# One row of a residual RMSNorm's second tile, dealt out unevenly to the DMA engines in patches of single partitions

## Chip, cores, metric

One core of one Trainium2 chip. The metric is the device time of one execution in microseconds (us), the median of several runs; runs of one kernel here mostly agree within 0.3%.

## The reference

```python
# x, residual: (32, 2048, 2048) float32; gamma: (2048,); eps = 1e-6
z = x + residual
rms = np.sqrt(np.mean(z ** 2, axis=-1, keepdims=True) + eps)
return (z / rms * gamma).astype(np.float32)
```

There are 65,536 rows of 8 KB. Each is read twice (x and residual) and written once: 1.61 GB in all.

## The kernel before

Rows go through in tiles of 128 partitions. Tile 0 has three rows in each partition, tile 1 five, and 72 further tiles seven each. Two buffers `z` (x, then the sum, then the result) alternate, and `r_area` holds residuals. SyncE issues every transfer; VectorE adds and scales; ScalarE squares and sums. GpSimd only clears the semaphores at the end.

```python
lead = [3, 5]
sizes = lead + [R] * n_full                       # R = 7
def rows(t, i):                                   # tile i of an HBM tensor
    k = sizes[i]
    return t[starts[i] : starts[i] + P * k, :].rearrange("(p r) m -> p r m", r=k)
...
def sp_turn(sp, t):                               # SyncE, for each tile i
    t.wait(sp, "done", -1)                        # tile i-1 computed
    ... dma_start(out=rows(o_f, i - 1), in_=z[...])        # store it
    t.wait(sp, "add_a")                           # first add of tile i done
    load_r(sp, t, 1)                              # residual of tile i+1
    t.wait(sp, "s_out", -1)                       # the store has landed
    load_x(sp, t, 1)                              # x of tile i+1
...
def sync_program(sp):
    load_x(sp, Turn(0)); load_r(sp, Turn(0))
    sp.wait_ge(tail_ev["add"], 1)                 # a memset of the gamma stage
    ... four loads of gamma
    load_r(sp, Turn(1)); load_x(sp, Turn(1))
    for i in range(1, n_tiles): sp_turn(sp, Turn(i))
    ... the last tile's stores, in four parts
```

Of the kernel before, what the change touches and what calls it, by code (L numbers as in the profile page):

```python
# [9 lines left out]
def kernel(  # L10
# [14 lines left out]



    nc = tc.nc
    P = nc.NUM_PARTITIONS
    fp32 = mybir.dt.float32  # L30
# [3 lines left out]
    x_f = x.flatten_outer_dims()  # L34
    r_f = residual.flatten_outer_dims()
    o_f = out.flatten_outer_dims()

    n_rows, D = x_f.shape
    R = 7
    STEP = 4  # L40
    U = 16
    lead = [3, 5]
    n_full = (n_rows // P - sum(lead)) // R
    sizes = lead + [R] * n_full
    starts = [0]
    for k in sizes:
        starts.append(starts[-1] + P * k)
    assert starts[-1] == n_rows
    n_tiles = len(sizes)
    last = n_tiles - 1  # L50

# [5 lines left out]
    def rows(t, i):  # L57
        k = sizes[i]
        return t[starts[i] : starts[i] + P * k, :].rearrange("(p r) m -> p r m", r=k)

    inv_d = 1.0 / float(D)

    def sb(name, shape):
        return ctx.enter_context(nc.sbuf_tensor(name, shape, fp32))
# [4 lines left out]
    sems = []  # L69

    def sem(name):
        sems.append(ctx.enter_context(nc.semaphore(name)))
        return sems[-1]
# [3 lines left out]
    z = [sb(f"z{p}", [P, R, D]) for p in range(2)]  # L77
    r_area = sb("r_area", [P, R + STEP, D])
    eps_tile = sb("eps_tile", [P, 1])
    ssq = [[sb(f"ssq{p}{h}", [P, 4]) for h in range(2)] for p in range(2)]  # L80
    rms = [[sb(f"rms{p}{h}", [P, 4]) for h in range(2)] for p in range(2)]
    rstd = [[sb(f"rstd{p}{h}", [P, 4]) for h in range(2)] for p in range(2)]
    tail_ssq = sb("tail_ssq", [P, R])
    tail_rms = sb("tail_rms", [P, R])
    tail_rstd = sb("tail_rstd", [P, R])
# [8 lines left out]
    dve = sem("dve_own")  # L94
    act = sem("act_own")
    s_tail = sem("s_tail")
    fin = sem("fin")
    tail_ev = {k: sem(f"tail_{k}") for k in ("add", "rms", "done")}


# [2 lines left out]
    def entry(i):  # L103
        if i == 0:
            return R + STEP - sizes[0]
        return 0 if i % 2 else STEP

    def parts(i):
        if i == 0:
            return [(0, 2), (2, sizes[0])]  # L110
        k = sizes[i] if i < 2 else R
        return [(STEP, k), (0, STEP)] if i % 2 else [(0, R - STEP), (R - STEP, R)]

    class Turn:

# [12 lines left out]
    def inc(ins, kind, i):  # L128
        return ins.then_inc(ev[kind][i % 2], U)


    def load_x(sp, t, d=0):
        i = t.i + d
        inc(sp.dma_start(out=z[i % 2][:, : sizes[i], :], in_=rows(x_f, i)), "x_in", i)

    def load_r(sp, t, d=0):
        i = t.i + d
        e = entry(i)
        inc(
            sp.dma_start(out=r_area[:, e : e + sizes[i], :], in_=rows(r_f, i)),  # L140
            "r_in",
            i,
        )

    def sp_turn(sp, t):
        i = t.i
        t.wait(sp, "done", -1)
        inc(
            sp.dma_start(out=rows(o_f, i - 1), in_=z[(i - 1) % 2][:, : sizes[i - 1], :]),
            "s_out",  # L150
            i - 1,
        )
        if i == last:
            return
        t.wait(sp, "add_a")
        load_r(sp, t, 1)
        t.wait(sp, "s_out", -1)
        if i + 1 == last:
            for k, (a, b) in enumerate(tail):
                sp.dma_start(  # L160
                    out=z[last % 2][:, a:b, :], in_=rows(x_f, last)[:, a:b, :]
                ).then_inc(x_tail[k], U)
        else:
            load_x(sp, t, 1)


    def add(v, i, a, b):
        e = entry(i)
        s = z[i % 2][:, a:b, :]
        return v.tensor_add(out=s, in0=s, in1=r_area[:, e + a : e + b, :])  # L170

    def scale(v, i, a, b, rs, c=0):
        for g in range(a, b):
            s = z[i % 2][:, g, :]
            ins = v.scalar_tensor_tensor(  # L175
                out=s,
                in0=s,
                scalar=rs[:, c + g - a : c + g - a + 1],
                in1=gamma_tile[:, :],
                op0=mult,  # L180
                op1=mult,
            )
        return ins

    def dve_turn(v, t, own):
        i, p = t.i, t.p
        t.wait(v, "x_in")
        t.wait(v, "r_in")
        (a0, b0), (a1, b1) = parts(i)
        inc(add(v, i, a0, b0), "add_a", i)  # L190
        inc(add(v, i, a1, b1), "add_b", i)
        for h, (a, b) in enumerate(parts(i)):
            n = b - a
            t.wait(v, "rms_a" if h == 0 else "rms_b")
            v.reciprocal(out=rstd[p][h][:, :n], in_=rms[p][h][:, :n]).then_inc(dve, U)  # L195
            v.wait_ge(dve, own(i, h))
            ins = scale(v, i, a, b, rstd[p][h])
        inc(ins, "done", i)
# [44 lines left out]



    stage = r_area[:, 5:7, :].rearrange("p r m -> p (r m)")
    stage = stage.rearrange("p (a b) -> p a b", a=16)[:, :, : D // 16]

    def sync_program(sp):
        load_x(sp, Turn(0))  # L250
        load_r(sp, Turn(0))

        sp.wait_ge(tail_ev["add"], 1)
        for q in range(4):
            sp.dma_start(  # L255
                out=stage[32 * q : 32 * q + 1],
                in_=gamma.partition_broadcast(1).rearrange("p (a b) -> p a b", a=16),
            ).then_inc(g_in, U)
        load_r(sp, Turn(1))
        load_x(sp, Turn(1))  # L260
        for i in range(1, n_tiles):
            sp_turn(sp, Turn(i))
        for k, (a, b) in enumerate(tail):
            sp.wait_ge(tail_ev["done"], k + 1)
            sp.dma_start(
                out=rows(o_f, last)[:, a:b, :], in_=z[last % 2][:, a:b, :]
            ).then_inc(s_tail, U)

    def vector_program(v):
        v.memset(eps_tile[:, :], float(eps))  # L270
        v.memset(stage, 0.0).then_inc(tail_ev["add"], 1)  # L271
        v.wait_ge(g_in, 4 * U)
        v.stream_shuffle(gamma_tile[:, :].rearrange("p (a b) -> p a b", a=16), stage, [0] * 32)  # L273
        for i in range(LO):
            dve_turn(v, Turn(i), lambda i, h: (2 * i + h + 1) * U)
        with v.Fori(0, 2 * n_iter, 2) as it:
            for i in range(LO, LO + 2):
                dve_turn(v, Turn(i, it), lambda i, h: it * (2 * U) + (2 * i + h + 1) * U)
        for i in range(HI, last):
            dve_turn(v, Turn(i), lambda i, h: (2 * i + h + 1) * U)  # L280
        base = 2 * last * U
        t = Turn(last)
        t.wait(v, "r_in")

        def tail_scale(k):
            a, b = tail[k]
            v.wait_ge(tail_ev["rms"], k + 1)
            v.reciprocal(out=tail_rstd[:, a:b], in_=tail_rms[:, a:b]).then_inc(dve, U)  # L288
            v.wait_ge(dve, base + (k + 1) * U)
            scale(v, last, a, b, tail_rstd, a).then_inc(tail_ev["done"], 1)  # L290

        for k, (a, b) in enumerate(tail):
            v.wait_ge(x_tail[k], U)
            add(v, last, a, b).then_inc(tail_ev["add"], 1)
            if k:
                tail_scale(k - 1)
        tail_scale(len(tail) - 1)

    def scalar_program(s):
        chain = Chain(s, act)  # L300
        for i in range(LO):
            act_turn(s, Turn(i), chain)
        with s.Fori(0, 2 * n_iter, 2) as it:
            n = chain.n
            chain.base = it * R
            for i in range(LO, LO + 2):
                act_turn(s, Turn(i, it), chain)
            assert chain.n - n == 2 * R
        chain.base = None
        chain.n = n + 2 * R * n_iter  # L310
        for i in range(HI, last):
            act_turn(s, Turn(i), chain)
        for k, (a, b) in enumerate(tail):
            chain.wait()
            s.wait_ge(tail_ev["add"], k + 2)
            act_part(
                s, chain, z[last % 2], a, b, tail_ssq[:, a:b], tail_rms[:, a:b]
            ).then_inc(tail_ev["rms"], 1)

    sync_program(nc.sync)  # L320
    vector_program(nc.vector)
    scalar_program(nc.scalar)

    nc.gpsimd.wait_ge(ev["s_out"][(last - 1) % 2], ((last - 1) // 2 + 1) * U)
    nc.gpsimd.wait_ge(s_tail, U * len(tail))
    ids = [a.num for a in sems]
    assert ids == list(range(ids[0], ids[0] + len(ids)))
    nc.gpsimd.sem_clear(range(ids[0], ids[-1] + 1))


# [33 lines left out]
```

## Time and profile before

| | before |
|---|---|
| time, median (lowest to highest of 3) | 3726.32 us (3726.11 to 3726.45) |
| VectorE / ScalarE / GpSimd busy | 62% / 29% / 0% |
| DMA traffic over the span | 432 GB/s mean, 434 in mid-run |
| last stores: first and last of the final sixteen semaphore increments | 3717.03 and 3723.36 us |

The trace of before has sixteen increments of the semaphore for each transfer of 128 partitions (592 for the 37 loads of x into `z[0]`), and they are read here as one from each of the core's sixteen DMA engines when its share has landed. The trace also keeps one record for each packet (a packet here is the contiguous rows of one partition: 24 KB in tile 0, 40 KB in tile 1, 56 KB later) with its duration, but not the engine of a packet. One more table of stretches is needed. Its columns are the stretch, its length, busy time of VectorE, ScalarE and GpSimd (with instructions), the granted TensorE clock, the mean busy share of the DMA engines, and GB/s. The kernel before:

```profile
16.00:40.00 24.00, 16.01 (x9) 7.77 (x9) 0.00 (x0) 1.00 1.01 429
40.00:60.00 20.00, 13.31 (x4) 7.93 (x8) 0.00 (x0) 1.00 1.03 442
60.00:350.00 290.00, 180.42 (x62) 82.04 (x92) 0.00 (x0) 1.00 1.00 433
350.00:3600.00 3250.00, 2008.80 (x705) 934.74 (x1022) 0.00 (x0) 1.00 1.00 434
```

A share near 1 says that the engines always had a packet in hand. (A packet counts in the stretch in which it starts, so a share can pass 1.)

### The profile page before, as it was taken

To read this page: it belongs to the slowest core of one execution; us is meant where nothing else is said; L and a number is where in the kernel's file an instruction comes from. 1 tells how busy PE (TensorE), PEld (TensorE's weight loads), DVE (VectorE), ACT (ScalarE), POOL (GpSimd) and SP (SyncE) were. 2 spreads that over 40 slices of the span, in tenths; PEclk is the share of its full clock that TensorE was granted. 3 is DMA by queue.
4 is the path that set the end of the run, shared out by engine and by line. 5 is a ranking of instruction groups with operands and counts; after the bars stand their busy time and mean duration, and the time that the engine had idled before them with its cause. 6 is when DMAs were issued, how large, how long until landed. Compare 5 with 4: busy or idle time off the path is not lost.

```text
span 3724.5 us, 3677 instructions
## 1 busy us (share of the span) xinstructions
DVE 2302.6 (62%) x816; ACT 1072.4 (29%) x1176; POOL 0.2 (0%) x4
## 2 busy tenths in 40 slices
DVE  5666665566665566665566665566665566655566
ACT  2233322233322233322233322233322233322233
POOL 0000000000000000000000000000000000000000
DMA  9999999999999999999999999999999999999999
GB/s 421 431 434 434 433 434 436 434 434 434 434 434 434 434 434 434 434 434 434 434 434 434 434 434 434 434 434 434 434 434 434 434 434 434 434 434 434 434 433 399
DMA packets 32964, 1610.69 MB, mean 432 GB/s; under 512 B 3712, under 2 KB 3776, under 8 KB 3776
## 3 DMA queue, kind: packets, MB, share of 16 engines
q1 hardware_dynamic: 32960, 1610.66, 99.9%
q14 instruction: 4, 0.03, 0.0%
HBM read 1073.77 MB, written 536.87 MB: 432 GB/s over the span
## 4 chain that ended last, share of the span: by engine, by line
DMA 66%; DVE 22%; issue 10%; ACT 1%; SPq 0%; DVEq 0%; ACTq 0%
DMA out_dram<-z 33%; DMA z<-in_x_dram 33%; DVE z L170 15%; DVE z L175 7%; ACT sq_junk L221 1%; DMA r_area<-in_gamma_dram 0%; ACT rms L229 0%; DVE rstd L195 0%; DVEq L126 0%; SPq L255 0%; DVE r_area L271 0%; ACTq L209 0%; ACTq L126 0%; DVE tail_rstd L288 0%; SPq L160 0%
## 5 line engine op out<-in xcount | busy, mean ns | idle before, releaser
L170 DVE TENSOR_TENSOR z<-z,r_area 128x8192 f32<-128x8192 f32 (+2 forms) x150 | 1109.5, 7437 | 1253.0 <-DMA z<-in_x_dram 1226.8
L221 ACT ACTIVATE sq_junk<-z 128x2048 f32<-128x2048 f32 x512 | 963.4, 1882 | 2617.9 <-DVE z L170 2606.5
L175 DVE SCALAR_TENSOR_TENSOR z<-z,rstd,gamma_tile 128x2048 f32<-128x2048 f32 x505 | 1153.5, 2344 | 5.2
L195 DVE RECIPROCAL rstd<-rms 128x4 f32<-128x4 f32 (+2 forms) x146 | 25.3, 174 | 130.8 <-ACT rms L229 130.8
L221 ACT ACTIVATION_READ_ACCUMULATOR sq_junk<-z 128x1 f32 x512 | 95.4, 186 | 0.0
L229 ACT ACTIVATE rms<-ssq,eps_tile 128x4 f32<-128x4 f32 (+2 forms) x146 | 43.3, 297 | 13.4
L175 DVE SCALAR_TENSOR_TENSOR z<-z,tail_rstd,gamma_tile 128x2048 f32<-128x2048 f32 x7 | 16.2, 2346 | 0.1
L273 DVE LOAD_MASK_SELECT gamma_tile<-r_area x1 | 0.0, 14 | 16.4 <-DMA r_area<-in_gamma_dram 16.4
L273 DVE STREAM_SHUFFLE gamma_tile<-r_area 128x2048 f32<-128x2048 f32 x1 | 2.3, 2290 | 0.0
L271 DVE MEMSET r_area<- 128x2048 f32 x1 | 1.8, 1765 | 0.4 <-issue 0.4
L221 ACT ACT_TABLE_LOAD x1 | 1.3, 1283 | 0.9 <-SPq L75 0.9
L229 ACT ACT_TABLE_LOAD x1 | 1.3, 1283 | 0.1
L229 ACT ACTIVATE tail_rms<-tail_ssq,eps_tile 128x2 f32<-128x2 f32 (+1 forms) x4 | 1.2, 295 | 0.1
L270 DVE MEMSET eps_tile<- 128x1 f32 x1 | 0.1, 59 | 1.0 <-SPq L75 1.0
L288 DVE RECIPROCAL tail_rstd<-tail_rms 128x2 f32<-128x2 f32 (+1 forms) x4 | 0.6, 158 | 0.0
L345 POOL MEMSET const-bfloat16-1.0<- 128x1 bf16 x1 | 0.1, 102 | 0.0
L345 POOL MEMSET const-uint8-127<- 128x1 uint8 x1 | 0.1, 102 | 0.0
L345 POOL MEMSET const-float32-1.0<- 128x1 f32 x1 | 0.1, 99 | 0.0
L345 POOL MEMSET const-float32-0.0<- 128x1 f32 x1 | 0.1, 98 | 0.2 <-issue 0.2
## 6 DMA issues: line engine op xcount, KB each, us to landing
r_area<-in_residual_dram SPq DMA_DIRECT2D x72, 7168.0 KB, 27.2
z<-in_x_dram SPq DMA_DIRECT2D x71, 7168.0 KB, 33.8
out_dram<-z SPq DMA_DIRECT2D x71, 7168.0 KB, 34.4
z<-in_x_dram SPq DMA_DIRECT2D x3, 2048.0 KB, 26.3
out_dram<-z SPq DMA_DIRECT2D x3, 2048.0 KB, 14.1
r_area<-in_residual_dram SPq DMA_DIRECT2D x1, 5120.0 KB, 25.3
z<-in_x_dram SPq DMA_DIRECT2D x1, 5120.0 KB, 36.8
out_dram<-z SPq DMA_DIRECT2D x1, 5120.0 KB, 24.8
```

The costliest lines, as they stand in the source:

```text
L170: return v.tensor_add(out=s, in0=s, in1=r_area[:, e + a : e + b, :])
L175: ins = v.scalar_tensor_tensor(out=s, in0=s, scalar=rs[:, c + g - a : c + g - a + 1], in1=gamma_tile[:, :], op0=mult, op1=mult,)
L195: v.reciprocal(out=rstd[p][h][:, :n], in_=rms[p][h][:, :n]).then_inc(dve, U)
L221: s.activation(out=sq_junk[:, :], in_=src[:, g, :], func=Act.Square, accum_out=sq[:, g - a : g - a + 1],)
L229: return s.activation(out=rm, in_=sq[:, : b - a], func=Act.Sqrt, bias=eps_tile[:, :], scale=inv_d)
L270: v.memset(eps_tile[:, :], float(eps))
L271: v.memset(stage, 0.0).then_inc(tail_ev["add"], 1)
L273: v.stream_shuffle(gamma_tile[:, :].rearrange("p (a b) -> p a b", a=16), stage, [0] * 32)
L288: v.reciprocal(out=tail_rstd[:, a:b], in_=tail_rms[:, a:b]).then_inc(dve, U)
L345: nc = _bacc.Bacc("TRN2", target_bir_lowering=False, num_devices=1)
```

## The change

Its intent: some DMA engines end later than others, so give them fewer rows. Tile 1 keeps four rows in every partition. Its fifth row (128 rows of HBM) is dealt out in six patches. A patch `(e, n, j, r)` puts `r` rows into each of the `n` partitions `8e + j`, `8(e+1) + j`, and so on, eight apart, so that each is meant for one DMA engine. (The patch families lie on partitions two apart, `j` = 0, 2, 4.) SyncE issues three patches; GpSimd issues three, with tiny loads between them that are meant to turn the engine at which the next patch begins. Partitions without a patch hold zeros.

```diff
-    lead = [3, 5]
+    lead = [3, 4]
+    sp_patches = [(0, 16, 0, 3), (0, 4, 2, 3), (0, 3, 4, 3)]
+    pool_patches = [(5, 2, 4, 1), (8, 8, 4, 3), (5, 11, 2, 3)]
+    def patch_rows(t, q):                 # the patch's rows in HBM, one after the other
+        n = first_row[q]
+        return t[n : n + q[1] * q[3], :].rearrange("(p r) m -> p r m", r=q[3])
+    def patch(area, q):                   # its place in SBUF
+        e, n, j, r = q
+        p = 8 * e + j
+        return area[p : p + 8 * (n - 1) + 1 : 8, STEP : STEP + r, :]
 ...
+        for k, t, area in ((0, r_f, r_area), (1, x_f, z[1])):       # SyncE
+            sp.wait_ge(clean[k], 1)       # memset of three rows
+            for q in sp_patches:
+                sp.dma_start(out=patch(area, q), in_=patch_rows(t, q)).then_inc(m_in, U)
         load_r(sp, Turn(1))
         load_x(sp, Turn(1))
 ...
+                if n:                     # GpSimd: meant to turn the engine
+                    g.dma_start(out=tiny[:n, c], in_=x_f[:n, c]).then_inc(t_in[turn], U)
+                move(m, q)                # load, later store, of one patch
```

VectorE's first add of tile 1 waits for the patches alone. The store of tile 1 is followed by the patches' stores. (Left out: semaphores, a reset of GpSimd's queue, and gamma's stage, which moves from `r_area` to `z[0]`.)

More of the change, by code (lines that the diff above doesn't have):

```diff
@@ L41 @@
     U = 16
-    lead = [3, 5]
-    n_full = (n_rows // P - sum(lead)) // R
+    lead = [3, 4]
+    n_full = (n_rows // P - sum(lead) - 1) // R
     sizes = lead + [R] * n_full
     starts = [0]
-    for k in sizes:
-        starts.append(starts[-1] + P * k)
+    for i, k in enumerate(sizes):
+        starts.append(starts[-1] + P * k + (P if i == 1 else 0))
     assert starts[-1] == n_rows
+    sp_patches = [(0, 16, 0, 3), (0, 4, 2, 3), (0, 3, 4, 3)]
+    pool_patches = [(5, 2, 4, 1), (8, 8, 4, 3), (5, 11, 2, 3)]
+    first_row = {}
+    n = starts[1] + P * sizes[1]
+    for q in sp_patches + pool_patches:
+        first_row[q] = n
+        n += q[1] * q[3]
+    assert n == starts[2]
     n_tiles = len(sizes)
@@ L82 @@
     rstd = [[sb(f"rstd{p}{h}", [P, 4]) for h in range(2)] for p in range(2)]
+    tiny = sb("tiny", [16, 64])
     tail_ssq = sb("tail_ssq", [P, R])
@@ L96 @@
     s_tail = sem("s_tail")
-    fin = sem("fin")
+    clean = [sem(f"clean{k}") for k in range(2)]
+    m_in = sem("m_in")
+    m_out = sem("m_out")
+    n_q = len(pool_patches)
+    q_in = [sem(f"q_in{k}") for k in range(2 * n_q)]
+    q_out = [sem(f"q_out{k}") for k in range(n_q)]
+    t_in = [sem(f"t_in{k}") for k in range(3 * n_q)]
     tail_ev = {k: sem(f"tail_{k}") for k in ("add", "rms", "done")}
@@ L110, in parts @@
             return [(0, 2), (2, sizes[0])]
-        k = sizes[i] if i < 2 else R
-        return [(STEP, k), (0, STEP)] if i % 2 else [(0, R - STEP), (R - STEP, R)]
+        return [(STEP, R), (0, STEP)] if i % 2 else [(0, R - STEP), (R - STEP, R)]
     class Turn:
@@ L152, in sp_turn @@
         )
+        if i == 2:
+            for q in sp_patches:
+                sp.dma_start(out=patch_rows(o_f, q), in_=patch(z[1], q)).then_inc(m_out, U)
         if i == last:
@@ L157, in sp_turn @@
         t.wait(sp, "s_out", -1)
+        if i == 2:
+            sp.wait_ge(m_out, len(sp_patches) * U)
+            for k in q_out:
+                sp.wait_ge(k, U)
         if i + 1 == last:
@@ L186, in dve_turn @@
         i, p = t.i, t.p
-        t.wait(v, "x_in")
-        t.wait(v, "r_in")
+        if i == 1:
+            v.wait_ge(m_in, 2 * len(sp_patches) * U)
+            for k in q_in:
+                v.wait_ge(k, U)
+        else:
+            t.wait(v, "x_in")
+            t.wait(v, "r_in")
         (a0, b0), (a1, b1) = parts(i)
         inc(add(v, i, a0, b0), "add_a", i)
+        if i == 1:
+            t.wait(v, "x_in")
+            t.wait(v, "r_in")
         inc(add(v, i, a1, b1), "add_b", i)
@@ L242, in act_turn @@
             )
-    stage = r_area[:, 5:7, :].rearrange("p r m -> p (r m)")
+    stage = z[0][:, 3:5, :].rearrange("p r m -> p (r m)")
     stage = stage.rearrange("p (a b) -> p a b", a=16)[:, :, : D // 16]
@@ L258, in sync_program @@
             ).then_inc(g_in, U)
+        for k, t, area in ((0, r_f, r_area), (1, x_f, z[1])):
+            sp.wait_ge(clean[k], 1)
+            for q in sp_patches:
+                sp.dma_start(out=patch(area, q), in_=patch_rows(t, q)).then_inc(m_in, U)
         load_r(sp, Turn(1))
@@ L271, in vector_program @@
         v.memset(stage, 0.0).then_inc(tail_ev["add"], 1)
+        v.memset(r_area[:, STEP:R, :], 0.0).then_inc(clean[0], 1)
         v.wait_ge(g_in, 4 * U)
@@ L318, in scalar_program, with pool_program, patches @@
             ).then_inc(tail_ev["rms"], 1)
+    def pool_program(g):
+        g.memset(z[1][:, STEP:R, :], 0.0).then_inc(clean[1], 1)
+        turn = 0
+        g.wait_ge(clean[0], 1)
+        g.wait_ge(clean[1], 1)
+        def patches(move):
+            nonlocal turn
+            at = 0
+            for m, q in enumerate(pool_patches):
+                n = (q[0] - at) % 16
+                if n:
+                    c = slice(4 * turn, 4 * turn + (4 if n > 1 else 1))
+                    g.dma_start(out=tiny[:n, c], in_=x_f[:n, c]).then_inc(t_in[turn], U)
+                    turn += 1
+                move(m, q)
+                at = (q[0] + q[1]) % 16
+            assert at == 0
+        for k, t, area in ((0, r_f, r_area), (n_q, x_f, z[1])):
+            patches(
+                lambda m, q: g.dma_start(
+                    out=patch(area, q), in_=patch_rows(t, q)
+                ).then_inc(q_in[k + m], U)
+            )
+        Turn(1).wait(g, "done")
+        patches(
+            lambda m, q: g.dma_start(
+                out=patch_rows(o_f, q), in_=patch(z[1], q)
+            ).then_inc(q_out[m], U)
+        )
+        for k in q_in + q_out + t_in[:turn]:
+            g.wait_ge(k, U)
     sync_program(nc.sync)
+    pool_program(nc.gpsimd)
     vector_program(nc.vector)
     scalar_program(nc.scalar)
+    ids = [a.num for a in sems]
+    assert ids == list(range(ids[0], ids[0] + len(ids)))
+    nc.gpsimd.dma_reset(range(ids[0], ids[-1] + 1))
     nc.gpsimd.wait_ge(ev["s_out"][(last - 1) % 2], ((last - 1) // 2 + 1) * U)
     nc.gpsimd.wait_ge(s_tail, U * len(tail))
-    ids = [a.num for a in sems]
-    assert ids == list(range(ids[0], ids[0] + len(ids)))
     nc.gpsimd.sem_clear(range(ids[0], ids[-1] + 1))
```

## The prediction

> **What bounds the kernel now.** I read the page first for the share of each engine and of the DMA engines, then a table of five stretches, then the order of time at both ends of the run, and last the times at which the DMA engines raised the semaphores.
>
> ```profile
> DVE 2302.6 (62%) x816; ACT 1072.4 (29%) x1176; POOL 0.2 (0%) x4
> ...
> DMA  9999999999999999999999999999999999999999
> GB/s 421 431 434 434 433 434 436 434 434 434 434 434 434 434 434 434 434 434 434 434 434 434 434 434 434 434 434 434 434 434 434 434 434 434 434 434 434 434 433 399
> ...
> q1 hardware_dynamic: 32960, 1610.66, 99.9%
> ```
>
> VectorE is busy 62% of the span, ScalarE 29%, GpSimd nothing. The one DMA queue is busy 99.9% of sixteen engines' span, at a level 434 GB/s from the third slice on. The transfers set the time, and no arithmetic can be saved to any effect.
>
> ```profile
> core 0: us, DVE busy (x) ACT busy (x) POOL busy (x), PEclk, DMA share, GB/s
> 0.00:20.00 20.00, 2.23 (x4) 1.28 (x1) 0.20 (x4) 1.00 0.93 380
> 20.00:60.00 40.00, 28.92 (x12) 15.71 (x17) 0.00 (x0) 1.00 1.01 435
> 60.00:3640.00 3580.00, 2209.81 (x776) 1025.59 (x1125) 0.00 (x0) 1.00 1.00 434
> 3640.00:3700.00 60.00, 52.12 (x20) 27.52 (x31) 0.00 (x0) 1.00 1.00 430
> 3700.00:3725.00 25.00, 9.49 (x7) 2.29 (x3) 0.00 (x0) 1.00 0.70 298
> ```
>
> The share column is the point: 1.00 everywhere but 0.93 in the first 20 us and 0.70 in the last 25. The last stretch lacks 0.30 x 25 = 7.5 us of sixteen engines' work, though stores are still waiting:
>
> ```profile
> 3691.17 18.76 SPq L265 DMA_DIRECT2D out_dram<-z  x4
> ...
> 3707.02 0.16 DVE L288 RECIPROCAL tail_rstd<-tail_rms 128x1 f32<-128x1 f32 x1
> 3707.22 2.35 DVE L175 SCALAR_TENSOR_TENSOR z<-z,tail_rstd,gamma_tile 128x2048 f32<-128x2048 f32 x1
> ```
>
> The last compute instruction ends at 3709.57 and the last store is issued then, yet the span ends at 3724.5. One row per partition takes an engine eight packets of about 0.302 us, 2.4 us. So something stands in a queue for over ten microseconds. The trace's record of semaphore increments says what: a transfer raises its semaphore sixteen times, once for each engine. For the last store these come from 3717.03 on, about ten of them within half a microsecond, one at 3717.89, then 3719.51, 3719.83, 3719.99, 3721.06 and 3723.36. The span ends 1.15 us after the last of these. Set against the first, that is five engines late by 2.5 to 6.3 us. The same pattern stands in the loads: the residual load that lands near 17.7 us has a spread of 1.1 us, near 265 us 2.6, near 1179 us 3.9, near 3615 us 6.4. Thus some engines fall slowly behind through the whole run, and **the one that is furthest behind sets the end**. The others stand idle for up to 6 us. An engine that never stalls would need 3 x 4096 rows at 2116 ns per packet of seven rows (the median in the trace), 302.3 ns a row: 3714.5 us, from a first packet at 1.97 us to 3716.5. The leading engines do just that.
>
> [...]
>
> **The change part by part.** The total is the same: tile 1 has four rows per partition in place of five, and the fifth (128 rows) goes in six patches. [...]SyncE gives 3 rows to all sixteen, 3 more to engines 0 to 3, 3 more to 0 to 2; GpSimd gives 1 to engines 5 and 6, 3 to 8 to 15 and 3 to 5 to 15. So 0 to 2 get 9, 3 gets 6, 4 gets 3, 5 and 6 get 7, 7 gets 6, 8 to 15 get 9: 27+6+3+14+6+72 = 128. Each had 8. Every row is moved three times (x, residual, output), so in packets of 302.3 ns:
> engine 4: 15 fewer, -4.53 us; engines 3 and 7: 6 fewer, -1.81; engines 5 and 6: 3 fewer, -0.91; the eleven others: 3 more, +0.91.
> Five engines are unburdened and five are late: the trace doesn't name the engine of a packet, and I choose to read the deal as the author's measure of it, engine 4 being the last. Then the ends are: leaders 3717.0 + 0.91 = 3717.9; the one at 3717.89, 3718.8; engine 4 3723.36 - 4.53 = 3718.83; the second, 3721.06, less 1.81 or 0.91 = 3719.25 or 3720.15; the rest at or below 3719.1. The latest is 3719.3 to 3720.2 against 3723.36: **a gain of 3.2 to 4.1 us** if nothing else moves. The mean of the sixteen ends stays near 3718.5, so more than 4.9 is not there.
>
> Against it stands the start, where engine 4 can run dry.
>
> ```profile
> 1.47 1.76 DVE L271 MEMSET r_area<- 128x2048 f32 x1 [0.40 <-issue]
> 3.26 2.51 SPq L255 DMA_DIRECT2D r_area<-in_gamma_dram  x4
> ...
> 19.60 2.29 DVE L273 STREAM_SHUFFLE gamma_tile<-r_area 128x2048 f32<-128x2048 f32 x1
> ...
> 39.41 0.35 SPq L149 DMA_DIRECT2D out_dram<-z  x1
> 43.31 10.89 DVE L170 TENSOR_TENSOR z<-z,r_area 128x2048 f32<-128x2048 f32 x2 [3.92 <-DMA z<-in_x_dram]
> ...
> 72.25 0.34 SPq L149 DMA_DIRECT2D out_dram<-z  x1
> 84.92 15.16 DVE L170 TENSOR_TENSOR z<-z,r_area 128x6144 f32<-128x6144 f32 x2 [12.70 <-issue]
> ```
>
> The new memset of three rows costs 3 x 1.76 = 5.3 us by that first row and ends near 8.6; SyncE then issues six patches of some 0.63 us (a quarter of 2.51) and the two loads by about 13.4. The queue holds tile 0 until 17.5, so SyncE costs nothing. GpSimd starts near 8.6 too, with 12 small transfers; its first patches go in between the packets of tile 0, up to two of 0.91 us on engines 8 to 15 before gamma lands[...]. Tile 0's store therefore goes out at about 41 in place of 39.4, its first packet about a microsecond later (0.95 to 1.97 at the start). Until then an ordinary engine has work up to 42.3 + 0.6 = 42.9, so it just doesn't run dry. Engine 4 has ten rows fewer by then, 3.0 us: dry at 39.2 to 40.3, idle for 1.5 to 2.5 us. What is idle there is lost of its 4.5, so it ends near 3720.3 to 3721.3. Engines 3 and 7 lose up to 1 us in the same way.
>
> The rest lies beside other work. VectorE adds two rows more (4.4 us) and scales two more (4.7), ScalarE squares two more (4.1), mostly of zeros; but the first add of tile 1 no longer waits for the loads, so the next residual load is asked for near 47 instead of 45.6, and the store of tile 1 some 2 to 4 us later than 72.25. Nothing waits for it until 84.9. The closing waits of GpSimd and its reset are done by about 100 us. The sum: -4.1 to -3.2 for the balance, +0.5 to +1.5 for the dry start, about **-3 us**, 3723.3.
>
> **The rivals.** First, the lag makes itself anew: packets over 100 ns too long add up to 18 us in the trace, nearly all between 50 and 535 us, as if engines that run in step get in each other's way until they are apart. Then engine 4, sent ahead by 4.5 us, may fall back to a place of its own, and the end is anywhere from 3721 to 3728. For it speaks that lags rise fast at first and then rest (3.9 us from 1000 to 2500); against it that one engine drifts on to 6.4, and that three runs agree within 0.34 us. Second, GpSimd's patches land on other engines than meant: [...]engine 4 would get 9 rows: 0.91 us later, 3727.2. The small dummy transfers[...] look tested, which speaks against it. Third, GpSimd is slow to issue and VectorE waits for its patches: it has from 8.6 to about 41, 2.7 us for each of 12[...]. At 4 us each all engines would idle some 15 us and the time would be about 3740. Fourth, SyncE's third load waits for all patches of the store; they have from 75 to 97 us, enough.
>
> **Range and chances.** 3723.3, with 3720.5 (full gain and luck) to 3727.2 (second rival). Two per cent is 74 us, which neither the balance nor any start of a few dozen microseconds reaches: same 0.99.
>
> **What would show it.** In the changed profile the last stretch's DMA share should rise, the increments of the last store should lie within 2 to 4 us, and the last load of tile 0 should land 1 to 2 us later. If the spread is still 6 us, the deal or the mechanism is wrong; if the first 60 us show a DMA share well below 1, the start ate the gain; a first add of tile 1 that waits on a GpSimd patch would be the third rival.

Cut from it, and marked, is what no run of this case shows: the paragraph on a ceiling of the traffic and on how transfers are divided among the engines, and phrases on the same and on how long a transfer of GpSimd takes. Two things were estimates, shown by no trace at the time. The rows of each engine are counted as the kernel's source means them, `e` being the first engine of a patch; the change's trace bears that out for SyncE and refutes it for GpSimd (below). And "up to two of 0.91 us" in front of gamma rested on a time of issue that no trace had; in the change GpSimd needs 0.52 us for each issue, and two of its 8 KB packets, of 0.309 us, do start before 17 us, while tile 0 is still loading (its last increment comes at 18.84). The second rival's nine rows for engine 4 count one partition for each engine from the first on, in each patch of eight partitions or more; that too was shown only afterwards, by the increments of `own_late`.

## The result, and the profile after

| | before | after |
|---|---|---|
| time, median of 4 (lowest to highest) | 3726.39 us (3726.11 to 3727.19) | 3741.05 us (3738.28 to 3744.16) |
| ratio, 95% interval | 1 | 1.0039 (1.0022 to 1.0057) |

The prediction was 3723.3, with 3720.5 to 3727.2. The change is within 2% of before, and clearly 14.7 us slower. A ratio here and below is the mean time of one kernel's fast runs over that of the other's of the same rounds, so not quite the ratio of the medians quoted.

The page of the changed kernel, the lines that answer to those in the prediction:

```profile
DVE 2316.5 (62%) x819; ACT 1076.4 (29%) x1180; POOL 14.9 (0%) x23
...
DMA  9999999999999999999999999999999999999999
GB/s 370 416 425 424 435 435 435 431 433 435 436 431 433 433 436 433 432 433 437 433 432 432 438 433 431 433 438 434 431 433 434 437 432 432 435 436 433 432 433 398
...
q0 software_dynamic: 576, 1.45, 0.2%
```

The DMA line is all nines as before, but the first four slices of 93.6 us carry 370, 416, 425 and 424 GB/s where before had 421, 431, 434 and 434. The loss is over in 400 us. Queue 0 is GpSimd's. The same stretches as above, the changed kernel:

```profile
16.00:40.00 24.00, 11.19 (x6) 7.77 (x9) 0.33 (x1) 1.00 1.02 237
40.00:60.00 20.00, 14.32 (x6) 6.30 (x7) 0.00 (x0) 1.00 1.01 433
60.00:350.00 290.00, 178.97 (x65) 81.38 (x89) 3.14 (x6) 1.00 1.00 422
350.00:3600.00 3250.00, 2010.31 (x704) 935.25 (x1024) 0.00 (x0) 1.00 1.00 434
```

From 16 to 40 us the engines moved 237 GB/s instead of 429, with a share of 1.02. They were not dry: **they were busy, and slow**. In time at 434 GB/s that is (429 - 237) x 24 / 434 = 10.6 us. From 60 to 350 us it is 11 x 290 / 434 = 7.4 us more, and 0.4 between. The sum, 18.4, is about the 17.9 by which this profiled run (3744.16) lies above the profiled run of before (3726.29).

What the packets say. Between 16 and 40 us the trace has 37 packets of 24 KB on GpSimd's queue, of 1.95 us in the mean, and 97 packets of 32 KB (tile 1's ordinary loads, which are no patches) of 2.01 us. Elsewhere they take 0.91 us (tile 0 of either kernel) and 1.22 us (`row_pool`). From 60 to 350 us, packets of 56 KB take longer than their usual 2116 ns by 6.1 us in sum for each engine (before: 0.85). They do it in bursts at the end of a load, when the leading engines turn to the next store: at 138.4 us, for instance, sixteen packets in a row took 2.84 to 3.53 us. Both kernels have such bursts, small ones before (no packet over 2.88 us from 60 to 350 us; 3.73 in the change). After the patches' store the engines were 9 us apart (the residual load of tile 3 landed between 123.9 and 133.3 us; 112.6 and 113.9 before).

The order of time of the changed kernel, to set against the last fence of the prediction:

```profile
9.68 2.07 SPq L304 DMA_DIRECT2D r_area<-in_residual_dram  x3
...
25.13 2.29 DVE L320 STREAM_SHUFFLE gamma_tile<-z 128x2048 f32<-128x2048 f32 x1
...
44.84 6.55 DVE L204 TENSOR_TENSOR z<-z,r_area 128x6144 f32<-128x6144 f32 x1
44.95 0.35 SPq L176 DMA_DIRECT2D out_dram<-z  x1
...
56.97 8.69 DVE L204 TENSOR_TENSOR z<-z,r_area 128x8192 f32<-128x8192 f32 x1 [5.58 <-DMA z<-in_x_dram]
...
98.41 15.16 DVE L204 TENSOR_TENSOR z<-z,r_area 128x6144 f32<-128x6144 f32 x2 [14.73 <-issue]
```

Gamma is there at 25.13 instead of 19.60, tile 0's store is issued at 44.95 instead of 39.41, and tile 2's add starts at 98.41 instead of 84.92. The add of the patches (44.84) followed its predecessor without waiting for them.

The transfers by issue, the changed kernel (KB, then us from issue to landing):

```profile
r_area<-in_residual_dram POOLq DMA_DIRECT2D x1, 264.0 KB, 12.1
z<-in_x_dram POOLq DMA_DIRECT2D x1, 264.0 KB, 28.4
out_dram<-z POOLq DMA_DIRECT2D x1, 264.0 KB, 21.5
```

GpSimd issued quickly (about 0.52 us for each, all twelve by 16.4 us), but a patch of 264 KB took 12 to 28 us to land.

And the end: the final sixteen increments of the last stores run from 3734.64 to 3741.12 us, 6.5 us apart; before they were 6.3 apart. The balance that the deal was for did not come either.

### The profile page after: what moved, and what is told of

It is laid out like the page before. It is cut to its first block, busy times and chain, and to the rows that moved or that the text cites. A ratio compares the mean times of both kernels' runs of the same rounds, so it can differ in the third digit from the quotient of the medians.

```text
span 3742.4 us, 3730 instructions
## 1 busy us (share of the span) xinstructions
DVE 2316.5 (62%) x819; ACT 1076.4 (29%) x1180; POOL 14.9 (0%) x23
## 4 chain that ended last, share of the span: by engine, by line
DMA 67%; DVE 22%; issue 9%; ACT 1%; SPq 0%; DVEq 0%; ACTq 0%
DMA out_dram<-z 33%; DMA z<-in_x_dram 33%; DVE z L204 15%; DVE z L209 7%; ACT sq_junk L263 1%; DMA z<-in_gamma_dram 1%; ACT rms L271 0%; DVE rstd L237 0%; DVEq L153 0%; SPq L297 0%; DVE z L317 0%; SPq L182 0%; ACTq L251 0%; ACTq L153 0%; DVE tail_rstd L335 0%
## 5 line engine op out<-in xcount | busy, mean ns | idle before, releaser
L271 ACT ACTIVATE rms<-ssq,eps_tile 128x4 f32<-128x4 f32 (+2 forms) x146 | 43.3, 297 | 13.4
```

The source lines that it names most:

```text
L271: return s.activation(out=rm, in_=sq[:, : b - a], func=Act.Sqrt, bias=eps_tile[:, :], scale=inv_d)
```

## The experiments

Four theories were set against each other first. P: the partitions that a patch writes make it slow. Q: a second queue slows both. R: the four-row tile itself is to blame. U: the unevenness is. From the expectations, the mechanisms that P and, further on, S, S1 and S2 named have been cut, since no trace shows them; the cuts are marked, and what each theory expected stands.

Engines are numbered by SyncE's small transfers: one of n partitions, up to sixteen, is taken to use engines 0 to n - 1, one partition on each. No record names an engine, but packets can be strung into engines (see "The deal itself"). In the change's strings up to 36 us, three hold six of SyncE's patch packets, one holds four, and the others at most three, ties included: by the numbering it should be six for engines 0 to 2 (patches of 16, 4 and 3 partitions, residual and x), four for engine 3 and two for the rest. Which partitions of an ordinary transfer an engine writes is not shown.

In all the kernels of the table below, tile 1 is split, cleared and added as in the change; only the patches differ. A patch is written (first partition, count, step, rows).

| kernel | median, us | above before, us | GB/s 16-40 / 40-60 / 60-350 us |
|---|---|---|---|
| the change | 3741.05 | 14.7 | 237 / 433 / 422 |
| row_sp | 3726.89 | 0.5 | 430 / 438 / 433 |
| even8_sp | 3732.67 | 6.3 | 342 / 431 / 431 |
| even7_sp | 3732.74 | 6.3 | 345 / 442 / 432 |
| even8_wide | 3732.81 | 6.5 | 342 / 434 / 431 |
| row_pool | 3729.12 | 2.7 | 436 / 415 / 431 |
| even8_pool | 3739.13 | 12.8 | 317 / 388 / 428 |
| k8_own (one run) | 3735.63 | 9.3 | 398 / 433 / 425 |
| k8_rot (one run) | 3736.39 | 10.1 | 387 / 442 / 425 |
| k8_step8 (one run) | 3747.71 | 21.4 | 249 / 436 / 419 |

### An ordinary transfer, even patches, and the second queue

`row_sp`: the row as one ordinary transfer.

```diff
-    sp_patches = [(0, 16, 0, 3), (0, 4, 2, 3), (0, 3, 4, 3)]
-    pool_patches = [(5, 2, 4, 1), (8, 8, 4, 3), (5, 11, 2, 3)]
+    sp_patches = [(0, 128, 1, 1)]
+    pool_patches = []
```

> The fifth row of tile 1 goes as one ordinary 128-partition transfer (8 rows for each engine) from SyncE; GpSimd issues no transfer. Same memsets, same 4+3 row halves of tile 1. Theory P[...] and theory Q (the second queue, GpSimd's) both expect about the time of before, 3725 to 3728. Theory R (the four-row tile with its 32 KB pitch, or the later store of tile 0, costs it) expects about 3735 or more here too.

Measured 3726.89, ratio 1.0000 (0.9984 to 1.0017). R is out: the four-row tile, the memsets and the added arithmetic cost about half a microsecond.

`even8_sp`: patches of sixteen partitions eight apart, all from SyncE.

```diff
+    sp_patches = [(0, 16, 8, 3), (2, 16, 8, 3), (4, 16, 8, 2)]
+    pool_patches = []
```

> The row goes in three patches of sixteen partitions, eight apart, all from SyncE: every engine gets 8 rows, GpSimd issues nothing. P expects 3732 to 3740 and packets of 24 KB near 1.8 us in place of 0.91 while the patches are in flight. Q expects 3725 to 3728 and 0.91 us packets. A theory U (uneven dealing itself is the harm) also expects 3725 to 3728.

Measured 3732.67, ratio 1.0016; 24 KB packets of 1.5 to 2.0 us once tile 0 is in. The stretches of `row_sp` and of `even8_sp`, which move the same rows with as many rows for each engine:

```profile
16.00:40.00 24.00, 16.98 (x10) 7.77 (x9) 0.00 (x0) 1.00 1.02 430
```

```profile
16.00:40.00 24.00, 15.51 (x9) 7.77 (x9) 0.00 (x0) 1.00 1.02 342
```

The share is 1.02 in both and the traffic 430 against 342: the patches' shape alone, with one queue and an even deal, costs 6.3 us. Q and U can't be the whole.

`even7_sp`: steps of seven.

```diff
-    sp_patches = [(0, 16, 8, 3), (2, 16, 8, 3), (4, 16, 8, 2)]
+    sp_patches = [(0, 16, 7, 3), (2, 16, 7, 3), (4, 16, 7, 2)]
```

> As even8_sp, but the sixteen partitions of a patch are seven apart[...]. P expects at least half of the loss of even8_sp to vanish (3726 to 3730, packets mostly at 0.91 us). Q, U: 3725 to 3728, equal to even8_sp.[...]

Measured 3732.74, the same as `even8_sp`, and from 18 us on all the 24 KB patches took 1.53 to 1.86 us. P as I had put it missed: seven apart should have taken away at least half of the loss of eight apart.

`row_pool`: the ordinary transfer of `row_sp`, issued by GpSimd.

```diff
+    sp_patches = []
+    pool_patches = [(0, 128, 1, 1)]
```

> The row goes as one ordinary 128-partition transfer each way, but from GpSimd, so that its queue runs beside SyncE's; no patches, no dummies. P expects 3725 to 3728. Q expects 3732 or more, with packets of both queues longer than their size gives (over 1.3 times) between 12 and 40 us.

Measured 3729.12, ratio 1.0007. The expected number (3732) was not reached and its sign did not show: the packets of both queues kept their durations (8 KB 0.32 us, 24 KB 0.91, 32 KB 1.22). What cost 2.7 us is another thing. GpSimd's rows go in front of tile 0's, so that tile 0's store is issued at 42.31, and the engines run dry. The stretches of `row_pool`:

```profile
16.00:40.00 24.00, 13.72 (x9) 7.77 (x9) 0.00 (x0) 1.00 1.02 436
40.00:60.00 20.00, 19.96 (x6) 8.82 (x10) 0.00 (x0) 1.00 1.00 415
```

In its packet records the gap is plain: from 40 to 44 us 238 GB/s were moved with the engines busy 0.56 of the time. This is the dry start of the prediction, at its true size for an ordinary transfer.

`even8_pool`: the patches of `even8_sp`, issued by GpSimd.

> even8_sp with its three patches issued by GpSimd: even deal, sixteen engines[...]. If the second queue adds what row_pool showed (2.7) to what even8_sp showed (6.3), about 3735.4. If slow patches in a second queue also slow the ordinary packets of tile 0 that they run beside, 3738 or more, near the change (3741).

Measured 3739.13, ratio 1.0034 (1.0018 to 1.0051): 12.8 us above before, more than 6.3 + 2.7. Its patches run beside tile 0's ordinary packets and slow them (24 KB on SyncE's queue 1.37 us in the mean); gamma is there at 31.28 us and tile 0's store late, so that the queues run dry from 48 to 52 us (104 GB/s). **This even deal costs nearly as much as the change** (14.7), and the times of the two overlap (3738.58 to 3739.41, and 3738.28 to 3744.16). The 1.9 us between their medians are not the price of the unevenness: in `k8_own` below (one run) an uneven deal costs 9.3 us by itself.

### What makes a patch slow: HBM side or SBUF side

`even8_wide`: `even8_sp` with the rows of a patch 64 KB apart in HBM.

```diff
-        n = first_row[q]
-        return t[n : n + q[1] * q[3], :].rearrange("(p r) m -> p r m", r=q[3])
+        a = q[0] * 3 // 2
+        n = starts[2] - P
+        return t[n : n + P, :].rearrange("(p r) m -> p r m", r=8)[:, a : a + q[3], :]
```

> even8_sp with one thing changed: the rows that the sixteen partitions of a patch hold lie eight rows (64 KB) apart in HBM, as in row_sp, in place of three rows (24 KB). SBUF side, packets and order are those of even8_sp. Theory H (sixteen engines that read one short stretch of HBM, 384 KB, get in each other's way) expects 24 KB packets near 0.91 us and a time of 3726 to 3728. Theory S (the SBUF side of a patch is slow[...]) expects packets near 1.7 us and 3731 to 3734, as even8_sp (3732.7).

Measured 3732.81, as `even8_sp`: H is out.

`k8_own` and `k8_step8`: eight engines only, eight partitions in a patch, four or eight apart.

```diff
+    sp_patches = [(0,8,4,3),(1,8,4,3),(2,8,4,3),(3,8,4,3),(32,8,4,3),(33,8,4,1)]   # k8_own
+    sp_patches = [(0,8,8,3),(1,8,8,3),(2,8,8,3),(3,8,8,3),(4,8,8,3),(5,8,8,1)]     # k8_step8
```

> Only eight engines take patches, of eight partitions four apart (0, 4 .. 28)[...]. HBM rows packed as in even8_sp (192 KB a patch). S expects 24 KB packets near 0.91 us, H near or above 1.7 us. The time itself will be several us worse than before in either case (16 rows for each of eight engines, none for the others).

> As k8_own, but the eight partitions lie eight apart (0, 8 .. 56)[...]. S expects packets near 1.8 us while k8_own has 0.91; H expects the same duration in both.

The stretch of `k8_own`, then of `k8_step8`:

```profile
16.00:40.00 24.00, 16.80 (x10) 7.77 (x9) 0.00 (x0) 1.00 0.96 398
```

```profile
16.00:40.00 24.00, 15.66 (x9) 7.77 (x9) 0.00 (x0) 1.00 0.98 249
```

Between 18 and 40 us the patches of `k8_own` took 0.912 us nearly all, the longest 1.26; those of `k8_step8` 1.56 to 2.00. The same rows, the same deal, patches of eight partitions from SyncE and the same number of bytes in a packet in both: only the partitions differ, and the times are 3735.63 and 3747.71 (one run each, 12 us apart; the expectation of `k8_own` held, "several us worse" because eight engines carry it all: eight rows more for each, moved three times at 302.3 ns, are 7.3 us, an estimate). S holds (the SBUF side of a patch is slow), with the spacing as what differs; why, no trace says. And there is more than S said: in `k8_step8` the 32 KB packets, which are ordinary loads, took 1.95 us in the mean (1.25 in `k8_own`), up to 2.5 while, by the count of the queue, only engines 8 to 15 can have been at them. By that count, patches eight apart slow engines that have no part in them.

`k8_rot`: `k8_own` begun four partitions later. S1: only the spacing counts. S2: each engine is fast on particular partitions alone, those of `k8_own`.

```diff
+    sp_patches = [(4,8,4,3),(5,8,4,3),(6,8,4,3),(7,8,4,3),(36,8,4,3),(37,8,4,1)]
```

> As k8_own, but the partitions begin four later (4, 8 .. 32 in place of 0, 4 .. 28)[...]. Theory S1[...] expects 24 KB packets near 0.91 us as in k8_own and about 3735.6; theory S2[...] expects 1.5 to 1.9 us as in k8_step8 and about 3747.

Measured 3736.39, 24 KB packets of 0.95 us in the mean. S1 holds and S2 falls: beginning four partitions later costs 0.8 us here (3736.39 against 3735.63), and in these three kernels, of one run each, eight apart in place of four is what hurts (12 us). `even7_sp` does not fit a rule made of this: seven apart was as slow as eight.

### Does one slow pair suffice?

The kernel before with four unused loads of two partitions, two rows each, into rows of `z[1]` that tile 1 doesn't use:

```diff
+        for p, n, step in [(0,2,1),(2,2,1),(32,2,1),(34,2,1)]:      # pair_same: side by side
+        #                  [(0,2,4),(1,2,4),(2,2,4),(3,2,4)]        # pair_own: four apart
+            sp.dma_start(out=z[1][p : p + step * (n - 1) + 1 : step, 5:7, :], in_=...)
```

In the first of the two, the outcomes set against each other are that a slow pair holds up all engines (the ordinary packets at 2 us or more), and that it holds up itself alone (they stay at 1.52).

> The kernel before with four unused loads of two partitions (16 KB each, by engines 0 and 1) in front of tile 1's[...]. [...]the ordinary 40 KB packets of the fourteen other engines that run beside them go from 1.52 us to 2 or more, and x1 lands 2 to 5 us later than in pair_own. If sharing hurts only those that share, the others stay at 1.52 and only two engines are late.

> The same four loads, but on partitions 0 to 3 by engine 0 and 4 to 7 by engine 1[...]. Expected: all packets at their usual duration (16 KB 0.61 us, 40 KB 1.52 us), engines 0 and 1 later by 8 packets of a row, 2.4 us.

The 16 KB packets of the pair took 1.23 us side by side and 0.67 four apart, 1.8 times as long. But the 40 KB packets, nearly all of the others, stayed at 1.546 us in the mean (1.527 in `pair_own`), and x of tile 1 began to land at 42.4 us (42.1). Only the two engines of the pair were late, by 5.2 us (3.1 in `pair_own`). So one slow pair does not slow the others; eight engines eight apart do (`k8_step8`). Where between these it begins, why side by side is slow, and why seven apart is as bad as eight, stays open: what slow neighbours have in common is not shown, and no rule for partitions follows from these runs.

### The deal itself, on partitions four apart

`own_deal`: the change's rows for each engine exactly, as meant, on partitions four apart: from 0 up for engines 0 to 7, from 64 up for engines 8 to 15. Expected was that, if the placing carries the loss, the packets come back to 0.91 us. This needs five patches from GpSimd in place of three. `own_late`: the same, meant to leave engine 4 alone unburdened, and GpSimd waits for tile 0 and gamma.

```diff
+    sp_patches = [(0, 8, 0, 3), (1, 4, 0, 3), (2, 3, 0, 3)]                                          # own_deal
+    pool_patches = [(22, 2, 5, 1), (64, 8, 8, 3), (21, 3, 5, 3), (65, 8, 8, 3), (66, 8, 8, 3)]
+    # (first partition, count, first engine as meant, rows); partitions 4 apart
+    sp_patches = [(0, 5, 0, 3), (1, 4, 0, 3), (2, 4, 0, 2), (3, 2, 0, 1)]                            # own_late
+    pool_patches = [(20, 3, 5, 3), (64, 8, 8, 3), (21, 3, 5, 3), (65, 8, 8, 3), (22, 3, 5, 3), (66, 8, 8, 2)]
+        Turn(0).wait(g, "r_in"); g.wait_ge(g_in, 4 * U)                                              # own_late
```

> The deal of the change, engine for engine (9, 9, 9, 6, 3, 7, 7, 6, then 9 for each of 8 to 15)[...]. [...]packets of 24 KB come back to 0.91 us and the time to 3723 to 3728: before, plus up to 3 us for GpSimd's patches in front of tile 0 as in row_pool, less up to 3 us for engine 4. If unevenness or the second queue carries most of it, the time stays above 3734.

> A version that may beat both: [...]engine 4 alone unburdened (3 rows; the others 8 or 9), and GpSimd waits for tile 0 and gamma to land before it issues, so that tile 0 isn't delayed. Expected 3722 to 3724.5 if engine 4 is the late one in most runs and the start doesn't run dry; 3726 or more if either fails.

Both missed: 3746.96 (ratio 1.0054) and 3754.38 (1.0075). The order of time of `own_late`:

```profile
28.58 1.03 POOL L390 DMA_DIRECT2D z<-in_x_dram  x2
...
39.48 0.35 SPq L175 DMA_DIRECT2D out_dram<-z  x1
66.08 15.16 DVE L203 TENSOR_TENSOR z<-z,r_area 128x6144 f32<-128x6144 f32 x2 [26.64 <-DMA z<-in_x_dram]
```

Tile 0's store is back at 39.48, as in the kernel before, and then VectorE stands for 26.64 us, until the last patch that GpSimd issued before 29.6 has landed at 66. In these 36 us its queue got one to eight packets of 24 KB through in every 4 us.

**GpSimd's patches had not gone to the engines they were meant for.** The semaphores show it. Of the loads of x, the last patch of three partitions (meant for engines 5 to 7) raised its last three increments at 64.48, 64.57 and 65.36 us, and the last one of eight (meant for 8 to 15) at 65.09, 65.17 and 65.96, each 0.6 us later, which is one packet of 16 KB (0.611). So the same three engines carried both. Five others carried the patch of eight alone (54.5 to 59.1 us), and eight had nothing to carry (done by 45.6). The packet records agree: a packet starts some 3 ns before the one before it on its engine ends, so that packets can be strung into engines, but for ties. In `own_late` three such strings have patches of both kinds until 65 us, and in them packets of the two queues alternate while both have any. In the change, the two 8 KB packets of x that were meant for engines 5 and 6 (begun at 24.51 and 25.00 us) stand in strings with six patch packets from SyncE, which only engines 0 to 2 have.

So what was seen is one partition for each engine from engine 0 on, whatever the tiny loads before it. If all of GpSimd's patches went so, which is inferred, the change gave 16 rows to engines 0 and 1, 15 to engine 2, 12 to engine 3, 9 to 4 to 7, 6 to 8 to 10, and 3 to 11 to 15. Its trace fits: x of tile 1 landed at 64.1 to 64.2 us from three engines, at 61.8 from one, and from 58.1 to 60.8 from the other twelve. `own_deal` and `own_late` loaded engines 0 to 2 still more (21 to 26 rows), and had engines 0 to 7 write the partitions meant for 8 to 15. So they test neither the placing nor the deal, and that their 24 KB packets took 1.53 us in `own_deal` (0.91 expected), four apart though they lie, can't be put down to one cause: queue, engines and partitions all differ from `k8_own`. They show the third rival of the prediction in its real form: slow to land, not to issue.

### Which engine is late, and does it matter?

Sixteen tiny loads of 1, 2 .. 16 partitions behind a residual load: by the numbering above, what the landings of the one of n partitions have over those of n - 1 is engine n - 1's time.

```diff
+        if i == 70:                                   # who_before; 8 and 70 in the two others
+            for n in range(1, 17):
+                sp.dma_start(out=probe_t[:n, c], in_=x_f[:n, c]).then_inc(pr[n - 1], U)
```

> The kernel before with sixteen tiny loads (8 bytes a partition) of 1, 2 .. 16 partitions behind the residual load of turn 70: [...]what its increments have over those of n - 1 is engine n - 1's time. Time within 1 us of before. If the deal of the change follows the lags, engine 4 is the last, and 3, 5, 6, 7 are the other late ones; if not, other engines are late and the deal gave rows to late ones.

> The kernel before with the same two sets of tiny loads. As in who_before, engine 4 last at turn 70 by 3 us or more; at turn 8 (near 430 us) engine 4 among the late ones but not yet alone. If another engine is last this time, the lags aren't fixed to engines, and no fixed deal can follow them.

> The changed kernel with the sixteen tiny loads behind the residual loads of turn 8 and of turn 70. If the deal worked on the balance as meant, engine 4 is among the first at turn 8 (about 5 us ahead of where the others put it) and still not the last at turn 70. If the lag makes itself anew (the first rival of the prediction), engine 4 is last again at turn 70. If the patches of SyncE set the order, engines 0 to 2 are last at turn 8.

Times 3728.12, 3729.48 and 3748.66 (one run each: 1.8 and 3.3 us above before, 7.6 above the change, more than I expected). Microseconds behind the first engine, worked out from the increments:

| kernel, turn | 0 | 1 | 2 | 3 | 4 | 5 | 6 | 7 | 8 | 14 | 15 | others |
|---|---|---|---|---|---|---|---|---|---|---|---|---|
| who_before, 70 | 0.4 | 0.6 | 3.1 | 2.3 | **6.7** | 0.5 | 0.0 | 1.0 | 1.6 | 3.2 | 2.3 | to 0.4 |
| who_early_late, 8 | 0.0 | 0.2 | 0.5 | 2.1 | 0.6 | 0.0 | 0.3 | 0.6 | 2.1 | 2.8 | 3.4 | to 0.3 |
| who_early_late, 70 | 2.2 | 2.3 | 1.9 | 4.5 | **7.5** | 1.0 | 1.6 | 1.7 | 3.0 | 2.8 | 3.7 | to 0.6 |
| who_after, 8 | 6.0 | 6.2 | **7.7** | 3.5 | 3.4 | 1.2 | 0.8 | 0.0 | 1.2 | 1.5 | 1.5 | to 2.4 |
| who_after, 70 | 4.6 | 4.7 | 5.7 | 3.2 | **7.5** | 0.0 | 0.5 | 0.3 | 0.1 | 0.9 | 0.6 | to 1.3 |

Engine 4 is the last at the end of all three, and it becomes so late in the run: at turn 8 of the kernel before it is only 0.6 us behind. The other late ones of the kernel before are 2, 3, 14 and 15, not 5, 6 and 7. In the changed kernel engines 0 to 2 are the last at turn 8, as the deal that landed has it. Engine 4, 3.4 us behind there, had nine rows by that count, one above its share, and not three; it falls to 7.5 later. What an engine 4 with fewer rows would do was never run.

`burden4` and `burden5`: the kernel before, with five unused loads of two rows, of four or of five partitions four apart.

```diff
+        for p, n, step in [(0,4,4),(1,4,4),(2,4,4),(3,4,4),(32,4,4)]:   # burden5: n = 5
+            sp.dma_start(out=z[1][p : p + step * (n - 1) + 1 : step, 5:7, :], in_=...)
```

> The kernel before with five unused loads of four partitions and two rows[...], in front of tile 1's: engines 0 to 3 each move ten rows more, 3.0 us. If the end is that of engine 4 and lags add up over the run, the time stays within 0.7 us of before (engine 2, 3 us behind at worst, comes up to engine 4's 6.7). If any delay of some engines delays all (the buffers wait for the last), up to 3 us more.

> The same with five partitions: engine 4 too moves ten rows more. If lags add up and engine 4 is the last, 3.0 us more than before, so that taking rows away could have gained as much; if engine 4's lag is one that it comes to wherever it starts (as who_after hints), 0 to 1 us, and the deal could gain nothing by its early rows.

Measured over five rounds: 3727.44 (3727.07 to 3728.29), ratio 1.0003, and 3731.30 (3730.87 to 3732.00), ratio 1.0013. Ten rows more for engines 0 to 3 cost 1.0 us; adding engine 4 costs 3.9 more, where ten rows are 3.0. (Both times lie above what was expected, 0.7 and 3.0 us over before.) So engine 4 sets the end, and rows that it carries in the first 60 us count in full at 3700. That taking rows from it would gain as much, up to the next late engine, is inferred: no kernel here took any.

## Why the prediction was wrong

- **The bound** (transfers; the engine furthest behind sets the end) was right: `burden4` against `burden5`.
- **The size of the prize** was right in kind: engine 4 is the last, and its rows count in full. My reading of the deal, as it was meant, held for engines 4 and 3 alone: engines 2, 14 and 15, also late, were given a row more, and engines 5, 6 and 7, which are not very late, were relieved.
- **The step that failed** is "Every row is moved three times (x, residual, output), so in packets of 302.3 ns". For the patches that term was mis-sized by two, and it was not confined to the patches: 24 KB took 1.95 us on GpSimd's queue instead of 0.907, and the ordinary 32 KB packets beside them 2.01 instead of 1.22. I took the duration of a packet from transfers of 128 partitions and applied it to patches of partitions eight apart, of which I had no trace. `k8_own` against `k8_step8` shows the effect for one queue: 0.95 and 1.64 us for the same packet.
- **A second step failed**: "GpSimd gives 1 to engines 5 and 6, 3 to 8 to 15 and 3 to 5 to 15". The patches landed on the lowest engines instead. By the increments' count engine 4 got nine rows and not three, so the -4.53 us on which the gain rests was never in the kernel; engines 0 and 1 got sixteen, which by the prediction's own 302.3 ns is +7.3 us (an estimate) where it has +0.91.
- **"+0.5 to +1.5 for the dry start"**: there was no dry start in the change (share 1.02 with 237 GB/s). Tile 0's store went out at 44.95, not 41, because the patches also slowed tile 0 and gamma. With an ordinary transfer in GpSimd's queue the dry start is real, 2.7 us (`row_pool`).
- **Times of issue**: GpSimd needs 0.52 us for a transfer; SyncE was done by 14.7, not 13.4. Neither held VectorE up.
- **The work on VectorE and ScalarE** was hidden, as predicted (`row_sp`: 0.5 us).
- **The rivals.** The first (the lag makes itself anew) is half right: engine 4 is last again, but the change lost its time before that. The second (other engines than meant) came true, and was taken too lightly: the prediction counted what it does to engine 4 (+0.91) and not to engines 0 to 2, and trusted the tiny loads because they "look tested". The third (VectorE waits for GpSimd's patches) did not happen in the change but did in `own_late`. That packets themselves might slow down was not on the list.

Two things thus went against the change, and the runs don't divide the 14.7 us between them. Slow packets in an even deal cost 6.3 us from one queue (`even8_sp`) and 12.8 from GpSimd's (`even8_pool`), of which a second queue without patches has 2.7 (`row_pool`); in the change itself they are seen at 16 to 40 us. An uneven deal with fast packets cost 9.3 (`k8_own`, sixteen rows for each of eight engines). Together they cost less than the sum of the two. Still open: why the long packets at the ends of loads go on to 350 us when the engines have come far apart (6.1 us for each engine in the change, 0.85 before, 1.3 in `even8_sp`).

## What to carry to other kernels

Before splitting a transfer into patches, measure the packets of one such patch. Here eight partitions four apart kept their speed (24 KB in 0.95 us in the mean, `k8_own`), and eight partitions eight apart took nearly twice as long (1.64, `k8_step8`) and slowed the traffic beside them (32 KB 1.95 us against 1.25). That is no rule of spacing: sixteen partitions seven apart were as slow as eight apart (`even7_sp`, 6.3 us over before, as `even8_sp`), and four apart from two queues took 1.53 (`own_deal`). Check GB/s beside the busy share; a share of 1.02 with 237 GB/s, where 429 went before, was a slow path and not a full one. A balance worth 3 us of a 3.7 ms run is worth having only if the rows that bring it are moved as well as all others, and late engines have to be found by measuring them, one by one. The same holds for the engines that rows were given to: look at the increments to see where a transfer from GpSimd has landed.
